# A hybrid decoder trunk on one core: which row pairs of a column pair take seven block products, and where three small pieces of work stand in the order

## The chip, the core and the metric

The kernel runs on one core of one Trainium2 chip. The metric is the device time of one execution in microseconds (us). The engines are TensorE (PE in the profile, its weight loads PEld), VectorE (DVE), ScalarE (ACT), GpSimd (POOL) and SyncE (SP, which here only issues DMAs).

## The reference

One sequence of 256 positions with 2048 features goes through two layers in float32. Layer 0 is retention with 8 heads (per head: 256 wide queries and keys, 512 wide values, a decay matrix, a norm, a SiLU gate), then a squared-ReLU MLP 2048 -> 8192 -> 2048. Layer 1 is latent attention with 16 heads, then such an MLP again.

```python
h = rms_norm(x, norm_mix[0]);  x = x + retention(h, ret_w_in, ret_w_out, cos, sin)
x = x + relu(rms_norm(x, norm_mlp[0]) @ w1[0])**2 @ w2[0]
k_nope, k_pe, v = mla_shared_kv(rms_norm(x, kv_norm_in), w_kv_down, ...)   # latent 512 + 64, up-projected
x = x + mla_attention(rms_norm(x, norm_mix[1]), w_dq, w_uq, w_o, k_nope, k_pe, v)
x = x + relu(rms_norm(x, norm_mlp[1]) @ w1[1])**2 @ w2[1]
```

Nearly all of the time is matrix products of the 256 rows with some 470 MB of float32 weights.

## The kernel before, in words

**Split products.** TensorE multiplies in a shorter float format. So each operand is split into a high and a low part (`split`, L164 to L173: ScalarE casts the high part, L167; VectorE subtracts it to get the low part, L168), and each product of a 128x128 with a 128x512 block is three matmuls (L336 to L338): high by high, high by low, low by high.

**Column pairs, eights and sevens.** The large products go by `gemm_pair` (L313): 1024 output columns (two blocks of 512) of all 256 rows (two blocks of 128). It runs over eight row pairs; each row pair is 256 rows of the weights, one DMA of 1 MB, and is worked on by `quad` (L264). A row pair is a 2x2 times 2x2 block product. Plainly that is 8 block products (24 matmuls, "an eight"): the 1 MB is split in two halves, two casts and two subtractions. With Strassen's and Winograd's scheme it is 7 (21 matmuls, "a seven"): then VectorE also adds the four weight blocks into sums u1 to u4 in place (L301, L304, L305), and four pieces are split instead of two (b11 with b22, b21, u1 with u2, u3 with u4; the second is half as long). A seven also needs sums of the blocks of the left operand, made once by `with_sums` (L372) and used by every column pair. `kinds` says which of the eight row pairs, counted from 0, are sevens. Results gather in seven PSUM banks; `pair_out` (L348) copies six of them (ScalarE) and adds them (VectorE), partly one step later.

**Which row pairs are sevens now.** `THREE` = 3, 5, 7; `FOUR` = 1, 3, 5, 7; `HEAD` = 3, 4, 6, 7 (L29). Heads 1 to 7 use HEAD in their gate-and-value pair (L754, named rp). The output projection of retention (ro) uses THREE and FOUR for the first four heads and 5, 7 for the last four. In the MLPs (L758 on) the up-projection (u) has eight column pairs p; p = 2, 4, 6 use FOUR, the others THREE, the first of layer 0 only 5, 7. Hidden features go in four groups: two u pairs, then two column pairs of the down-projection (d), the first with THREE and the second with FOUR; in the last group the first has THREE and the other 1024 columns are two plain products (`gemm`, L386) of one 512-wide block each. After a u pair, `up` (L765) adds the results, applies ReLU, transposes on TensorE, squares, splits, and makes the sums. After a d pair the results are added to the residual stream in HBM by DMA (`to_home`, L124), in the last group to the stream in SBUF (`into_x`, L132).

**Buffers.** 4 of raw weights, 5 of high halves and 5 of low halves (1024 columns each), 4 PSUM banks "acc", 2 "tp", 2 as one "at", 14 of 2 KB.

**Order.** Each chunk of weights is one tick of a clock (`tick`, L63). `later(n, fn)` puts work into a queue that is due n ticks later; `need` (L69) runs the queue until a list is long enough. Engines execute in order.

**Start.** Head 0 is done by plain products (rg, rq, rk, rv); its input blocks come in with the first of them (`start`, L588). The sums for HEAD are made from a second load of x (`again`, L563), due 7 + c ticks after block c came in; before head 1's pair, the queue is drained until all four are there (L752). GpSimd computes the angles of the two rotary tables (`sincos`, L465, some two dozen small steps each): retention's early, the latent attention's (named tm) due 12 ticks after the inputs, and its table (`mla_tables`, L515) 20 ticks after. They depend on positions only. GpSimd also makes each norm's reciprocal root (`rstd`, L142), the one of a head's output among them (`ret_out`, L644: `o_m`, `o_r`), for which VectorE's `y` (L660) waits.

**Between the layers.** `into_next` (L447) adds the last results to x, squares, transposes and scales it for the latent's down-projection (kd, 320 and 256 columns, L873) and the query's (dq). kd does its first block over all four chunks of rows, then its second. Before it, the queue is drained until the norm's root r2 is there (L816).

Of the kernel before, what the change touches and what calls it, by code (L numbers as in the profile page):

```python
# [19 lines left out]

P = 128
NT = 2
S = NT * P
D = 2048
KD = D // P
# [3 lines left out]
NOPE, ROPE, MV, KVR, QR = 128, 64, 128, 512, 1536  # L29
KV_NBS, Q_NB = (320, 256), 384  # L30
GROUPS = (4, 4, 4, 4)
THREE, FOUR, HEAD = (3, 5, 7), (1, 3, 5, 7), (3, 4, 6, 7)
PI = math.pi

G_MIX0, G_MLP0, G_KV, G_MIX1, G_MLP1 = 0, 16, 32, 48, 64
# [15 lines left out]
def yoco(ctx: ExitStack, tc: tile.TileContext, a):  # L51
# [29 lines left out]
    def later(n, fn):  # L81
        queue.append((clock[0] + n, next(count), fn))
# [327 lines left out]
    def x_block_t(blocks, b, g0s, outs, name, sums):  # L410

        for k2 in range(2):
            tp = transposed(
                lambda t, j: blocks[t][:, (2 * k2 + j) * P : (2 * k2 + j + 1) * P], f"{name}_tp{b}{k2}"
            )
            for g0, out in zip(g0s, outs):
                scales = [gain(g0 + b * 4 + k2 * 2 + j) for j in range(2)]
                v = act_tile(f"{name}{g0}_{b}{k2}")
                if not sums:
                    split_act(v, tp, scales)  # L420
                    out.append(v)
                elif 2 * b + k2 in FOUR:
                    u = f2k([2, S], f"{name}u_{b}{k2}")
                    for j in range(2):
                        nc.scalar.activation(u[:, j], tp[:, j], AF.Copy, scale=scales[j])
                    split_act(v, u)
                    out.append((v, with_sums(u, f"{name}{b}{k2}")))
                else:
                    split_act(v, tp, scales)
                    out.append((v, None))  # L430
# [31 lines left out]
    c1, c2, c3 = _pi_parts()  # L462
    pos_f = pool.tile([P, NT], F32, name="pos_f")

    def sincos(inv, w, name):  # L465

        n = NT * w

        def f2k(shape, name):
            return shaped(act_tile(name, F32).rearrange("p j i s -> p (j i s)"), shape)  # L470

        ang = f2k([NT, w], f"{name}_ang")
        for t in range(NT):
            nc.gpsimd.tensor_scalar(ang[:, t], inv, pos_f[:, t : t + 1], None, op0=ALU.mult)
        flat = ang.rearrange("p t w -> p (t w)")
        k = f2k([2, n], f"{name}_k")
        for i in range(2):
            nc.gpsimd.tensor_scalar(k[:, i], flat, 1 / (2 * PI), 0.25 * i, op0=ALU.mult, op1=ALU.add)
        nc.gpsimd.tensor_scalar(k, k, MAGIC, -MAGIC, op0=ALU.add, op1=ALU.add)
        kh = f2k([2, n], f"{name}_kh")  # L480
        nc.gpsimd.tensor_scalar(kh, k, MAGIC_HI, -MAGIC_HI, op0=ALU.add, op1=ALU.add)
        kl = f2k([2, n], f"{name}_kl")
        nc.gpsimd.tensor_tensor(kl, k, kh, op=ALU.subtract)
        r = f2k([2, n], f"{name}_rr")
        both = flat.unsqueeze(1).to_broadcast([P, 2, n])
        part = f2k([2, n], f"{name}_part")

        def less(dst, src, kk, c):
            nc.gpsimd.tensor_scalar(part, kk, c, None, op0=ALU.mult)
            nc.gpsimd.tensor_tensor(dst, src, part, op=ALU.subtract)  # L490
# [62 lines left out]
    def first_inputs(c):  # L553

        t = f2k([2, S], f"x0t_{c}")
        nc.sync.dma_start(t, a["xt"][:, 2 * c : 2 * c + 2, :])
        v = act_tile(f"a0_{c}")
        split_act(v, t, [gain(G_MIX0 + 2 * c + j) for j in range(2)])
        act0.append(v)
        sums0.append(None)  # L560
        if c in HEAD:

            def again():  # L563
                t = f2k([2, S], f"x0s_{c}")
                nc.sync.dma_start(t, a["xt"][:, 2 * c : 2 * c + 2, :])

                def sum_up():
                    for j in range(2):
                        nc.scalar.activation(t[:, j], t[:, j], AF.Copy, scale=gain(G_MIX0 + 2 * c + j))
                    sums0[c] = with_sums(t, f"a0s_{c}")  # L570

                later(2, sum_up)

            later(7 + c, again)

    ss0 = [small(NB, f"ss0_{t}") for t in range(NT)]

# [10 lines left out]
    def start(half):  # L588
        first_inputs(half)
        if half == 3:  # L590
            nc.sync.dma_start(pos_i, a["pos"])
            nc.sync.dma_start(cst, a["cst"])
            nc.sync.dma_start(gpe, a["gpe"])
        if half == 5:
            ret_tables()
        if half == 7:
            for b in range(NB):
                later(2 + b, lambda b=b: load_x(b))
            later(6, scale_tables)
            later(12, lambda: mla_sc.append(sincos(cst[:, C_INVM : C_INVM + 32], 32, "tm")))  # L600
            later(20, mla_tables)

    def ret_rope(acc, out, name, wait):

# [39 lines left out]
    def ret_out(h, s, v, gate, y_act):  # L644
# [10 lines left out]
        for t in range(NT):  # L655
            so = small(1, f"so{h}{t}")
            square_sum(o[:, t], so, f"o{h}{t}")
            ro = rstd(so, RDV, 1, f"o{h}{t}")
            y = f2k([512], f"y{h}{t}")
            nc.vector.scalar_tensor_tensor(y, o[:, t], ro, gate[t], op0=ALU.mult, op1=ALU.mult)  # L660
            ys.append(y)

        def turn():
            for k2 in range(2):
# [51 lines left out]
    for h in range(RH):  # L716
# [32 lines left out]
        if h == RH // 2:  # L749
            ret_out_half(0)  # L750
        need(r0, NT)
        while None in [sums0[k] for k in HEAD]:  # L752
            run_first()
        gemm_pair(a["ret_w_gv"], (h - 1) * 8, list(zip(act0, sums0)), [k in HEAD for k in range(8)], f"rp{h}", paired)  # L754
    ret_out_half(1)


    def mlp(layer, act, r, done):  # L758
        w1, w2 = a[f"mlp_w1_{layer}"], a[f"mlp_w2_{layer}"]
        f0 = 0  # L760
        for gi, nf in enumerate(GROUPS):
            hid, blocks = [], []
            last = gi == len(GROUPS) - 1

            def up(c, p, hid=hid, blocks=blocks, last=last):  # L765

                need(r, NT)
                c = summed(c)
# [4 lines left out]
                def turn(i):  # L773
                    for q in (2 * i, 2 * i + 1):
                        name = f"hid{layer}_{p}{q}"
                        tp = transposed(
                            lambda t, j: c[t][q // 2][:, (q % 2 * 2 + j) * P : (q % 2 * 2 + j + 1) * P], f"{name}_tp"
                        )
                        u = f2k([2, S], f"{name}_u")
                        nc.scalar.activation(u, tp, AF.Square)  # L780
                        v = act_tile(name)
                        split_act(v, u)
                        blocks.append((v, with_sums(u, name) if len(blocks) in (THREE if last else FOUR) else None))
                        hid.append(v)

                later(0, lambda: turn(0))
                later(1, lambda: turn(1))

            for p in range(f0 // 2, (f0 + nf) // 2):
                kinds = THREE[not (p or layer) :] if p % 2 or not p else FOUR  # L790
                gemm_pair(
                    w1, p * 8, act, [i in kinds for i in range(8)], f"u{layer}_{p}", lambda c, p=p, up=up: up(c, p)
                )
            if last:
                x_tiles(f"mlp{layer}")
            for p in range(2):
                if last and p:
                    for b in (2, 3):
                        need(hid, 2 * nf)
                        gemm(  # L800
                            a[f"mlp_w2t_{layer}"], (b - 2) * nf, hid, 4 * nf, 512, f"d{layer}_{gi}{b}",
                            lambda acc, b=b: done(b, acc),
                        )
                    continue

                def add(c, p=p, last=last):
                    into_x(done, c, p) if last else to_home(c, p)

                kinds = [i in (FOUR if p else THREE) for i in range(2 * nf)]
                gemm_pair(w2, p * 32 + 2 * f0, blocks, kinds, f"d{layer}_{gi}{p}", add)  # L810
            f0 += nf

    ss = [small(NB, f"ss2_{t}") for t in range(NT)]
    act_kv, act_q, r2 = [], [], []
    mlp(0, act, r, into_next(ss, [G_KV, G_MIX1], [act_kv, act_q], r2, "n2"))
    need(r2, 2)  # L816


    def pe_rope(dst, u, src, t, i, heads):
# [334 lines left out]
```

## Time and profile before

| what | us |
|---|---|
| three runs | 2496.07, 2493.91, 2493.17; median 2493.91 |
| the profiled execution, its own time | 2494.54 |
| span from its first to its last instruction | 2492.8 |
| TensorE busy / VectorE busy | 2466.3 / 2146.8 |
| retention, to the start of the first MLP | 0 to 745 |
| first MLP | 745 to 1428 |
| latent attention | 1428 to 1809 |
| second MLP | 1809 to 2490 |

How to read it: times in the trace are counted from the span's start. A row in order of time gives the start, the length, the engine, the line, what is written and read, and in brackets how long the engine stood idle before and what ended that. A row of a stretch gives its length and the busy time of each engine in it, then the granted clock of TensorE (1.00 is full), the busy share of the DMA engines and GB/s. The length of a matmul overlaps with the next; what counts is start to start. The records of VectorE overlap a little too.

### The profile page before, as it was taken

How to read it: one execution, taken by the hardware profiler on the slowest of the kernel's cores; microseconds unless marked ns; L12 is line 12 of the kernel's file. 1: busy time of each engine (PE TensorE's matmuls, PEld its weight loads, DVE VectorE, ACT ScalarE, POOL GpSimd, SP SyncE). 2: the span in 40 equal slices, each digit the busy share in tenths (PEclk: the TensorE clock that was granted, in tenths of full speed). 3: DMA queues.
4: the chain of work that ended last, by engine and by line, in shares of the span. 5: the costliest groups of instructions: out<-in, count | busy, mean ns of one | idle time of the engine just before them, and what ended most of it. 6: DMA issues, size and time to landing. Idle time of an engine off the chain costs nothing.

```text
span 2492.8 us, 31703 instructions
## 1 busy us (share of the span) xinstructions
PE 2466.3 (99%) x11644; PEld 2063.3 (83%) x11644; DVE 2146.8 (86%) x2782; ACT 1586.2 (64%) x2241; POOL 248.7 (10%) x308
## 2 busy tenths in 40 slices
PE   9999999999999999999999999999999999999999
PEld 7788888888788888888888888998888888888887
DVE  7798888889899999999999866776689999999996
ACT  6565655556577666667567666576566667576663
POOL 7300011000000020110110101111000201101100
PEclk9999999999999999999999999999999999999999
DMA  8555558456565595685785564445555866856854
GB/s 325 193 188 186 176 190 262 171 190 228 177 217 189 203 262 211 210 263 203 228 270 181 208 219 173 152 139 195 191 180 197 249 222 200 271 197 222 274 193 152
DMA packets 93403, 521.04 MB, mean 209 GB/s; under 512 B 11072, under 2 KB 12224, under 8 KB 40000
## 3 DMA queue, kind: packets, MB, share of 16 engines
q1 hardware_dynamic: 71856, 472.83, 52.4%
q0 software_dynamic: 21248, 46.15, 8.8%
q8 instruction: 91, 1.49, 0.2%
q14 instruction: 64, 0.52, 0.1%
q10 hardware_dynamic: 144, 0.05, 0.0%
HBM read 479.14 MB, written 39.85 MB: 208 GB/s over the span
## 4 chain that ended last, share of the span: by engine, by line
PE 90%; DVE 5%; ACT 3%; POOL 1%; issue 1%; DMA 0%; ACTq 0%; SPq 0%; DVEq 0%; POOLq 0%
PE u_c L336 7%; PE u_c L338 7%; PE u_c L337 7%; PE d_c L337 6%; PE d_c L338 6%; PE d_c L336 6%; PE rq_acc L256 2%; PE rp_c L336 2%; PE rp_c L337 2%; PE rp_c L338 2%; PE rk_acc L256 2%; PE u_p L336 2%; PE u_p L338 2%; PE u_p L337 2%; PE ro_c L338 2%; PE ro_c L336 2%
## 5 line engine op out<-in xcount | busy, mean ns | idle before, releaser
L167 ACT CAST u_wh<-u_raw 128x1024 fp32r<-128x1024 f32 x362 | 342.3, 991 | 213.8 <-DVE u_raw L304 141.7
L167 ACT CAST d_wh<-d_raw 128x1024 fp32r<-128x1024 f32 x352 | 333.4, 994 | 200.0 <-DVE d_raw L304 146.8
L168 DVE TENSOR_TENSOR u_wl<-u_raw,u_wh 128x1024 fp32r<-128x1024 f32 x362 | 396.9, 1143 | 51.8 <-ACT u_wh L167 50.7
L168 DVE TENSOR_TENSOR d_wl<-d_raw,d_wh 128x1024 fp32r<-128x1024 f32 x352 | 387.2, 1149 | 45.2 <-ACT d_wh L167 44.8
L336 PE MATMUL u_c<-u_wh,n 128*128 128x512 f32 x706 | 276.4, 392 | 0.0
L337 PE MATMUL u_c<-u_wl,n 128*128 128x512 f32 x706 | 275.6, 390 | 0.0
L338 PE MATMUL u_c<-u_wh,n 128*128 128x512 f32 x706 | 274.9, 389 | 0.0
L167 ACT CAST rp_wh<-rp_raw 128x1024 fp32r<-128x1024 f32 (+1 forms) x168 | 158.0, 978 | 128.0 <-DVE rp_raw L304 55.8
L336 PE MATMUL d_c<-d_wh,hid 128*128 128x512 f32 x608 | 238.1, 392 | 0.0
L337 PE MATMUL d_c<-d_wl,hid 128*128 128x512 f32 x608 | 237.5, 391 | 0.0
L338 PE MATMUL d_c<-d_wh,hid 128*128 128x512 f32 x608 | 236.7, 389 | 0.0
L168 DVE TENSOR_TENSOR rp_wl<-rp_raw,rp_wh 128x1024 fp32r<-128x1024 f32 (+1 forms) x168 | 183.1, 1132 | 36.8 <-ACT rp_wh L167 36.8
L338 PEld LDWEIGHTS u_c<-u_wh,n 128*128 128x128 f32 x706 | 132.6, 188 | 27.5
L336 PEld LDWEIGHTS u_c<-u_wh,n 128*128 128x128 f32 x706 | 132.5, 188 | 27.0
L337 PEld LDWEIGHTS u_c<-u_wl,n 128*128 128x128 f32 x706 | 132.6, 188 | 26.7
L338 PEld LDWEIGHTS d_c<-d_wh,hid 128*128 128x128 f32 x608 | 114.2, 188 | 23.5
L336 PEld LDWEIGHTS d_c<-d_wh,hid 128*128 128x128 f32 x608 | 114.2, 188 | 23.5
L337 PEld LDWEIGHTS d_c<-d_wl,hid 128*128 128x128 f32 x608 | 114.2, 188 | 22.9
L132 POOL DMA_DIRECT2D xh<-d_c x48 | 41.6, 867 | 855.5 <-ACT d_c L353 853.6
L167 ACT CAST ro_wh<-ro_raw 128x1024 fp32r<-128x1024 f32 x86 | 83.3, 999 | 59.4 <-PE ro_c L338 31.8
L336 PE MATMUL rp_c<-rp_wh,a 128*128 128x512 f32 x280 | 111.5, 398 | 6.0 <-DVE rk_u L608 4.5
L337 PE MATMUL rp_c<-rp_wl,a 128*128 128x512 f32 x280 | 109.8, 392 | 0.0
(463 smaller groups left out, 6147.4 us busy)
## 6 DMA issues: line engine op xcount, KB each, us to landing
u_raw<-in_mlp_w SPq DMA_DIRECT2D x128, 1024.0 KB, 5.7
d_raw<-in_mlp_w SPq DMA_DIRECT2D x112, 1024.0 KB, 5.2
rp_raw<-in_ret_w_gv SPq DMA_DIRECT2D x56, 1024.0 KB, 4.9
ro_raw<-in_ret_w_out SPq DMA_DIRECT2D x32, 1024.0 KB, 4.9
uq_raw<-in_mla_w_uq SPq DMA_DIRECT2D x24, 768.0 KB, 4.1
rq_raw<-in_ret_w_qk SPq DMA_DIRECT2D x16, 1024.0 KB, 5.7
rk_raw<-in_ret_w_qk SPq DMA_DIRECT2D x16, 1024.0 KB, 4.8
d_raw<-in_mlp_w2t SPq DMA_DIRECT2D x16, 1024.0 KB, 5.8
```

What stands on the lines that cost most here:

```text
L132: nc.gpsimd.dma_start(x_home[t][2 * p + j], part, accum_op=ALU.add)
L167: nc.scalar.copy(h, src)
L168: nc.vector.tensor_tensor(l, src, h.bitcast(F32), op=ALU.subtract)
L256: nc.tensor.matmul(acc[f], wh[:, cols], a.rearrange("p i s -> p (i s)"), start=k == 0, stop=k == nk - 1)
L336: nc.tensor.matmul(dst, ah, bh, start=n == 0, stop=False)
L337: nc.tensor.matmul(dst, ah, bl, start=False, stop=False)
L338: nc.tensor.matmul(dst, al, bh, start=False, stop=n == total[key] - 1)
```

## The change

Four parts:

1. In the MLPs every full u pair (p = 1 to 7) and both d pairs of the first three groups have four sevens, at 3, 4, 6, 7 (`LATE`); the first u pair of layer 0 has 6, 7, that of layer 1 has 4, 6, 7. Sums of hidden tiles and of x are made for these positions.
2. Heads 2 to 7 have their sevens at 2, 4, 6, 7, head 1 at 4, 6, 7; the second loads of x for them come later, each by its own number of ticks, and head 1's pair waits for each block's sums only when it gets to that block (`Pairs`).
3. The latent attention's table is computed after head 0's output root `ro`, tied to it by a zero that is made from it; the table itself 12 ticks after.
4. The last d pair of the first MLP is a column pair with sevens at 3, 5, 7; the second MLP keeps its plain products there. The latent's down-projection runs both column blocks over the first two chunks of rows and then both over the last two, and r2 is asked for only where its results are scaled.

```diff
+class Pairs:
+    def __init__(self, tiles, sums, kinds):
+        self.tiles, self.sums, self.kinds = tiles, sums, kinds
+    def __len__(self):
+        n = 0
+        while n < len(self.tiles) and (n not in self.kinds or self.sums[n] is not None):
+            n += 1
+        return n
+    def __getitem__(self, i):
+        return self.tiles[i], self.sums[i]
...
-THREE, FOUR, HEAD = (3, 5, 7), (1, 3, 5, 7), (3, 4, 6, 7)
+THREE, FOUR, HEAD = (3, 5, 7), (1, 3, 5, 7), (2, 4, 6, 7)
+LATE = (3, 4, 6, 7)
...
-                elif 2 * b + k2 in FOUR:
+                elif 2 * b + k2 in LATE:
...
-            later(7 + c, again)
+            later({2: 21, 4: 15, 6: 17, 7: 18}[c], again)
...
-            later(12, lambda: mla_sc.append(sincos(cst[:, C_INVM : C_INVM + 32], 32, "tm")))
-            later(20, mla_tables)
...
+        if h == 0:
+            no_move, pos = small(1, "no_move"), small(NT, "pos_m")
+            nc.gpsimd.tensor_scalar(no_move, ro, 0.0, None, op0=ALU.mult)
+            nc.gpsimd.tensor_scalar(pos, pos_f, no_move, None, op0=ALU.add)
+            mla_sc.append(sincos(cst[:, C_INVM : C_INVM + 32], 32, "tm", pos))
+            later(12, mla_tables)
...
-        while None in [sums0[k] for k in HEAD]:
-            run_first()
-        gemm_pair(a["ret_w_gv"], (h - 1) * 8, list(zip(act0, sums0)), [k in HEAD for k in range(8)], f"rp{h}", paired)
+        kinds = HEAD if h > 1 else HEAD[1:]
+        gemm_pair(
+            a["ret_w_gv"], (h - 1) * 8, Pairs(act0, sums0, kinds), [k in kinds for k in range(8)], f"rp{h}", paired
+        )
...
+            kinds = THREE if last else LATE
...
-                        blocks.append((v, with_sums(u, name) if len(blocks) in (THREE if last else FOUR) else None))
+                        blocks.append((v, with_sums(u, name) if len(blocks) in kinds else None))
...
-                kinds = THREE[not (p or layer) :] if p % 2 or not p else FOUR
+                sevens = LATE if p else LATE[2 - layer :]
...
-                if last and p:
+                if last and p and layer:
...
-                kinds = [i in (FOUR if p else THREE) for i in range(2 * nf)]
-                gemm_pair(w2, p * 32 + 2 * f0, blocks, kinds, f"d{layer}_{gi}{p}", add)
+                gemm_pair(
+                    w2, p * 32 + 2 * f0, blocks, [i in kinds for i in range(2 * nf)], f"d{layer}_{gi}{p}", add
+                )
...
-    need(r2, 2)
...
     def downed(acc, b):
+        need(r2, NT)
...
-    for b in range(2):
-        gemm(a[f"mla_w_kv_down_{b}"], 0, act_kv, KD, KV_NBS[b], f"kd{b}", lambda acc, b=b: downed(acc, b))
+    first = [accs(n, f"kd{b}") for b, n in enumerate(KV_NBS)]
+    for rows in (range(2), range(2, 4)):
+        for b, n in enumerate(KV_NBS):
+            for g in rows:
+                piece(
+                    a[f"mla_w_kv_down_{b}"], g, first[b], act_kv, g, KD, n, f"kd{b}",
+                    done=(lambda acc, b=b: downed(acc, b)) if g == 3 else None,
+                )
```

More of the change, by code (lines that the diff above doesn't have):

```diff
@@ L463, in yoco, with sincos @@
     pos_f = pool.tile([P, NT], F32, name="pos_f")
-    def sincos(inv, w, name):
+    def sincos(inv, w, name, pos_f=pos_f):
         n = NT * w
@@ L763, in mlp, with up @@
             last = gi == len(GROUPS) - 1
-            def up(c, p, hid=hid, blocks=blocks, last=last):
+            kinds = THREE if last else LATE
+            def up(c, p, hid=hid, blocks=blocks, kinds=kinds):
                 need(r, NT)
@@ L789, in mlp @@
             for p in range(f0 // 2, (f0 + nf) // 2):
-                kinds = THREE[not (p or layer) :] if p % 2 or not p else FOUR
+                sevens = LATE if p else LATE[2 - layer :]
                 gemm_pair(
-                    w1, p * 8, act, [i in kinds for i in range(8)], f"u{layer}_{p}", lambda c, p=p, up=up: up(c, p)
+                    w1, p * 8, act, [i in sevens for i in range(8)], f"u{layer}_{p}", lambda c, p=p, up=up: up(c, p)
                 )
@@ L800, in mlp @@
                         gemm(
-                            a[f"mlp_w2t_{layer}"], (b - 2) * nf, hid, 4 * nf, 512, f"d{layer}_{gi}{b}",
+                            a["mlp_w2t"], (b - 2) * nf, hid, 4 * nf, 512, f"d{layer}_{gi}{b}",
                             lambda acc, b=b: done(b, acc),
@@ L1140 @@
         arrays[f"mlp_w2_{i}"] = _quads(g["mlp_w2"][i])
-        arrays[f"mlp_w2t_{i}"] = _chunks(g["mlp_w2"][i][-512 * GROUPS[-1] :, 1024:], 512)
+    arrays["mlp_w2t"] = _chunks(g["mlp_w2"][1][-512 * GROUPS[-1] :, 1024:], 512)
     arrays = {n: np.ascontiguousarray(v) for n, v in arrays.items()}
```

## The prediction

> **What bounds the kernel now.** I read the page first, then busy time by stretch, then VectorE in order of time inside the MLP, then TensorE where it stands still.
>
> ```profile
> span 2492.8 us, 31703 instructions
> PE 2466.3 (99%) x11644; PEld 2063.3 (83%) x11644; DVE 2146.8 (86%) x2782; ACT 1586.2 (64%) x2241; POOL 248.7 (10%) x308
> PE 90%; DVE 5%; ACT 3%; POOL 1%; issue 1%; DMA 0%; ACTq 0%; SPq 0%; DVEq 0%; POOLq 0%
> ```
>
> TensorE carries the chain that ended last, so fewer products should mean less time. VectorE's 86% is an average over stages, though; in one MLP stretch (down-projection, two column pairs of one group) it reads otherwise:
>
> ```profile
> core 0: us, PE busy (x) PEld busy (x) DVE busy (x) ACT busy (x) POOL busy (x), PEclk, DMA share, GB/s
> 1001.00:1085.00 84.00, 84.00 (x380) 69.32 (x379) 78.83 (x91) 55.84 (x73) 9.37 (x11) 1.00 0.69 223
> 997.40:1040.90 43.50, 43.50 (x200) 35.84 (x200) 41.20 (x51) 31.14 (x42) 0.77 (x1) 1.00 0.52 193
> 1040.90:1081.80 40.90, 40.90 (x182) 33.81 (x181) 37.99 (x41) 25.06 (x31) 7.06 (x9) 1.00 0.86 258
> ```
>
> The last two rows are VectorE's own pair boundaries. The first pair has three sevens and also VectorE's work on the u pair before it (sums, hidden tiles): I call such a pair heavy. The second has four sevens and only a d pair's sums behind it: light. VectorE is busy 41.20 of 43.50 us and 37.99 of 40.90 us. Its remaining 2.3 and 2.9 us are no reserve, as these rows show (start, length):
>
> ```profile
> 1029.01 6.37 DVE L168 TENSOR_TENSOR d_wl<-d_raw,d_wh 128x1024 fp32r<-128x1024 f32 x6 [0.47 <-ACT d_wh L167]
> 1035.30 1.22 DVE L301 TENSOR_TENSOR d_raw<-d_raw 128x1024 f32<-128x1024 f32 x1
> 1036.55 0.69 DVE L304 TENSOR_TENSOR d_raw<-d_raw 128x512 f32<-128x512 f32 x1
> 1037.28 0.69 DVE L305 TENSOR_TENSOR d_raw<-d_raw 128x512 f32<-128x512 f32 x1
> 1038.44 2.36 DVE L168 TENSOR_TENSOR d_wl<-d_raw,d_wh 128x1024 fp32r<-128x1024 f32 x2 [0.47 <-ACT d_wh L167]
> ...
> 435.10 4.10 DVE L168 TENSOR_TENSOR rp_wl<-rp_raw,rp_wh 128x1024 fp32r<-128x1024 f32 x4 [0.58 <-ACT rp_wh L167]
> 439.11 1.22 DVE L301 TENSOR_TENSOR rp_raw<-rp_raw 128x1024 f32<-128x1024 f32 x1
> ...
> 442.25 2.36 DVE L168 TENSOR_TENSOR rp_wl<-rp_raw,rp_wh 128x1024 fp32r<-128x1024 f32 x2 [0.46 <-ACT rp_wh L167]
> ```
>
> Every seven ends with a wait of 0.47 us: L304 makes u2, ScalarE must cast it, and L305 is shorter than that cast.
>
> **The price of one seven.** On VectorE: two sevens side by side start 442.25 - 435.10 = 7.15 us apart. A seven and an eight take 1038.44 - 1029.01 = 9.43 us, so an eight takes 2.28, and making an eight a seven adds 4.87 us (4.4 work, 0.47 wait). On TensorE it takes away three matmuls:
>
> ```profile
> 1049.83 0.39 PE L336 MATMUL d_p<-d_wh,hid 128*128 128x512 f32 x1
> 1050.05 0.39 PE L337 MATMUL d_p<-d_wl,hid 128*128 128x512 f32 x1
> 1050.28 0.39 PE L338 MATMUL d_p<-d_wh,hid 128*128 128x512 f32 x1
> 1050.51 0.39 PE L336 MATMUL d_c<-d_wh,hid_more 128*128 128x512 f32 x1
> ```
>
> 1050.51 - 1049.83 = 0.68 us. From the code, before has 28 sevens in the heads, 11 in ret_out, 26 + 27 in the u pairs and 24 + 24 in the d pairs: 140. After: 27, 11, 30 + 31, 30 + 27: 156. Sixteen more take 10.9 us from TensorE and put 16 x 4.87 = 78 us on VectorE: one more in each of fourteen heavy pairs, three in the first MLP's last pair, one fewer in head 1.
>
> **Heavy pairs** (u pairs 1, 3, 5, 7 and the first d pair of three groups, two layers: 14). VectorE needs 41.20 + 4.4 + 4 x 0.47 = 47.5 us, and its other waits (about 0.9 us at the pair's end, behind ScalarE's copies of the sums) may stay. TensorE would need 43.5 - 0.68. VectorE sets the pair: 47.6 - 43.5 = +4.1 each, **+57**. Bounds: -0.68 each (-10, everything hidden) and +4.8 each (+67). The hidden tiles' sums only change sides (one for a group's first u pair, three for its second).
>
> **Light pairs** (12) keep four sevens, but move them from 1, 3, 5, 7 to 3, 4, 6, 7. The heads' pairs run those very positions today:
>
> ```profile
> 403.02 0.39 PE L336 MATMUL rp_c<-rp_wh,a 128*128 128x512 f32 x1
> ...
> 441.26 0.39 PE L338 MATMUL rp_c<-rp_wh,a 128*128 128x512 f32 x1
> 442.26 0.73 PE L336 MATMUL rp_p<-rp_wh,a0s_more 128*128 128x512 f32 x2 [0.62 <-ACT rp_wh L167]
> 443.21 0.50 PE L336 MATMUL rp_c<-rp_wh,a 128*128 128x512 f32 x1 [0.22 <-ACT rp_wh L167]
> ...
> 445.69 0.61 PE L256 MATMUL rq_acc<-a,rq_wh 128*128 128x512 f32 x2
> ```
>
> That pair takes 445.69 - 403.02 = 42.67 us for 180 matmuls that need 180 x 0.2267 = 40.81. It loses 1.9: two sevens in a row take VectorE 14.3 us and TensorE 2 x 21 x 0.2267 = 9.5, and the five buffers of split weights hold too little lead for that (lead: how long before TensorE uses a split half VectorE has made it). I take +1.9 each, **+23** (bounds 0 and +26). No lead is left for the heavy pair that follows, so its cost stands in full.
>
> **The other MLP pairs.** Last group's first d pair (three sevens as before) now starts without a lead: +1.5 twice. The first u pair of each layer has sevens 6 and 7 side by side: +0.5 twice. Both are estimates, parts of the light pair's 1.9. **+4** (0 to +8).
>
> **Last pair of the first MLP.** Three sevens replace a plain product of two blocks: -2.0 on TensorE.
>
> ```profile
> 1383.00:1428.00 45.00, 45.00 (x211) 37.04 (x210) 35.80 (x54) 29.34 (x55) 3.25 (x6) 1.00 0.56 197
> 1428.00:1455.00 27.00, 27.00 (x204) 26.90 (x203) 17.58 (x28) 18.31 (x35) 3.07 (x6) 1.00 0.71 241
> L171 DVE SCALAR_TENSOR_TENSOR n<-n_tp,gains,n 128x256 fp32r<-128x256 f32 x24 | 10.9, 478 | 2.5 <-ACT n L170 2.3
> ```
>
> VectorE has 9 us there. It gets 3 x 4.87 = 14.6 and 2.4 of pair sums, and loses about 4.4 (block 2's residual and an eighth, 8 of the 24 L171, moves behind the end): 48.2 for 45, +3. Behind it blocks 2 and 3 now arrive together. The reordered down-projection has four of its eight pieces, half of 27 us, to cover a chain of six ScalarE copies, four sums, four residual adds, transposes and eight scalings per block, with their subtractions: I take another +4. **+7** (-2 to +12). The reciprocal root r2 is needed only where `downed` scales, so its moved `need` costs nothing.
>
> **Heads.** Sevens at 2, 4, 6, 7 leave one neighbouring pair instead of two; of the 1.9 lost today I keep 0.15: 6 x -1.75 = **-10.5** (0 to -11.4). In head 1 the latent tables go:
>
> ```profile
> 95.70 0.19 POOL L145 TENSOR_SCALAR o_m<-so 128x1 f32<-128x1 f32 x1
> 96.51 0.47 POOL L490 TENSOR_TENSOR tm_rr<-tm_rr,tm_part 128x128 f32<-128x128 f32 x1
> DVE y L660 <- POOL o_r L147: 6.9, 2, 5.0
> 97.39 0.88 PE L187 MATMUL ytp<-cst,y 128*128 128x128 f32 x6 [1.29 <-DVE y L660]
> 110.01 0.50 PE L336 MATMUL rp_c<-rp_wh,a 128*128 128x512 f32 x1 [4.45 <-DVE rk_u L608]
> 105.00:115.00 10.00, 5.55 (x18) 4.08 (x17) 9.53 (x18) 6.53 (x11) 1.96 (x3) 0.83 0.70 261
> ```
>
> GpSimd runs the tables' steps around head 0's root o_m; VectorE waits 5.0 us for o_r and then holds the accumulator that rp needs. TensorE loses 1.3 + 4.5 us, and at a granted clock of 0.83 over ten microseconds another 1.7. Tied to that root, the steps come behind it: the same two dozen small ones on GpSimd and two more that carry the tie, one Sin on ScalarE, sixteen short products on VectorE. Behind them on GpSimd stands only head 1's root, a whole head away, so the added wait delays nobody. The four row-pair sums (ScalarE and VectorE) and their loads on SP, until now drained ahead of head 1's pair, are spread over its quads, of which one fewer is a seven (+0.7); the loads stand in SP's order with the weights', four buffers ahead. 7.5 - 0.7 plus 1.2 for the stalls that a seven fewer spares: **-8** (0 to -10).
>
> **Sum.** 57 + 23 + 4 + 7 - 10.5 - 8 = +72.5 on the profiled execution's 2494.5: 2567.0; the median shown lies 0.6 lower: **2566.4 us**.
>
> **Rivals.** (1) *VectorE absorbs it, faster*: if ordering fills ScalarE's waits, a stretch needs 78.83 + 4.4 = 83.2 us of 83.3 and TensorE stays the bound: 2494 - 10.9 - 18.5 = 2465. For it: TensorE never waits in the MLP today. Against: no seven in the rows above had its wait filled. It decides from where a stretch's waits stay under 0.1 us. Chance 0.13. (2) *Light pairs lend to heavy ones*: if the waits at the pairs' ends vanish and light pairs do not stall, a stretch takes 78.83 + 4.4 + 8 x 0.47 = 87.0 us, +3.0 instead of 4.1 + 1.9: 12 x 3.0 + 2 x 4.1 + 11 - 18.5 = +37, 2531. For it: the light pair's 37.99 of 40.90 leaves 1 us beside its four waits. Against: the heads' pairs stall at these positions today. Chance 0.17; 0.03 of it comes down to no difference. (3) *The clock falls too*:
>
> ```profile
> 1646.06 0.66 PE L187 MATMUL qptp<-cst,qpp 128*128 128x128 f32 x4 [1.88 <-DVE ot L168]
> 1643.00:1651.00 8.00, 6.12 (x37) 5.84 (x36) 5.17 (x12) 5.81 (x11) 2.31 (x1) 0.79 0.57 199
> ```
>
> A wait of 1.88 us was enough for a granted clock of 0.79 over the next 8 us, 1.7 us lost; a heavy pair's longest stall, at the second of two neighbouring sevens, I work out as 7.15 - 21 x 0.2267 = 2.4. Unless VectorE is then late anyway, 14 x 1.7 = +24: 2590. Chance 0.09. The Trainium skill (TensorE: Matmul & The Clock Gate, What's actually happening) says that the clock halves after an idle window of about 3.4 us; by that rule no heavy pair's stall would do it and this rival would be empty. The trace disagrees, with 1.88 us. That the sevens do not appear at all is no case: they are written out by index.
>
> **Chances.** Forecast 0.61 (its own range 2535 to 2588), rivals 0.13, 0.17, 0.09. Range 2505 to 2596: it leaves out rival 1, the low end of 2 and the top of 3. Within 0.2%, about what a measurement of this kernel can tell from no change, 0.03; faster 0.13; slower 0.84.
>
> **What would show it.** After the change the MLP stretches should be 88 to 92 us with VectorE over 93% busy and TensorE waiting for u_wh and d_wh; heads 2 to 7 shorter by about 1.7 each; no 4.5 us wait at 110; L660's wait for GpSimd under 2.5 us in head 0. I am wrong if VectorE fits into 83 us of a stretch, that is if L305's wait is filled, or if light pairs run at 40.9.

## The result, and the profile after

The kernel after takes 2562.16 us (median of 4 runs, 2560.70 to 2566.43); the kernel before, run beside it, 2494.07 (2493.17 to 2496.07). The ratio is 1.0275, 95% interval 1.0257 to 1.0293: 68.1 us slower.

Line numbers of this part move by 19: the casts are L186, the subtractions L187, the sums of a seven L320, L323, L324, the three matmuls L355 to L357. First the page of after, its span, busy times and chain:

```profile
span 2558.9 us, 31824 instructions
PE 2484.0 (97%) x11596; PEld 2043.5 (80%) x11596; DVE 2219.8 (87%) x2870; ACT 1605.1 (63%) x2279; POOL 249.2 (10%) x310
PE 73%; DVE 18%; ACT 6%; issue 2%; POOL 0%; DMA 0%; ACTq 0%; SPq 0%; DVEq 0%; POOLq 0%
```

VectorE's part of the chain went from 5% to 18%, while its share of the span rose by one point only. TensorE now waits, and these are its two largest sums of waits (us in total, times, longest):

```profile
PE d_p L355 <- ACT d_wh L186: 23.9, 24, 1.9
PE u_p L355 <- ACT u_wh L186: 18.8, 22, 1.0
```

The same group of the first MLP as in the prediction, at VectorE's pair boundaries (first the heavy d pair, its light one, then a light u pair and a heavy one):

```profile
1001.05:1049.92 48.87, 44.56 (x198) 34.85 (x196) 46.74 (x61) 32.87 (x46) 2.41 (x3) 1.00 0.55 183
1049.92:1093.11 43.19, 42.28 (x184) 33.85 (x183) 38.32 (x41) 24.90 (x31) 6.59 (x9) 1.00 0.78 238
1093.11:1135.99 42.88, 41.98 (x182) 33.38 (x181) 38.31 (x40) 24.89 (x31) 4.94 (x6) 1.00 0.77 239
1135.99:1182.20 46.21, 43.84 (x196) 34.48 (x194) 44.11 (x52) 31.59 (x44) 0.00 (x0) 1.00 0.51 183
```

The heavy pairs are 48.87 and 46.21 long, 47.54 in the mean (47.6 predicted; d has three of the hidden sums, u one). VectorE fills some 95% of them. The light pairs are 43.19 and 42.88, 2.1 over the 40.90 of before, and VectorE is *not* full there: 38.3, as before (37.99). Why they are longer all the same is seen in the light u pair. VectorE first, in order of time:

```profile
1100.18 4.09 DVE L187 TENSOR_TENSOR u_wl<-u_raw,u_wh 128x1024 fp32r<-128x1024 f32 x4
1104.19 1.22 DVE L320 TENSOR_TENSOR u_raw<-u_raw 128x1024 f32<-128x1024 f32 x1
...
1107.33 1.22 DVE L187 TENSOR_TENSOR u_wl<-u_raw,u_wh 128x1024 fp32r<-128x1024 f32 x1 [0.47 <-ACT u_wh L186]
1108.77 1.23 DVE L187 TENSOR_TENSOR u_wl<-u_raw,u_wh 128x1024 fp32r<-128x1024 f32 x1 [0.22 <-ACT u_wh L186]
1111.49 1.83 DVE L187 TENSOR_TENSOR u_wl<-u_raw,u_wh 128x1024 fp32r<-128x1024 f32 x2 [1.49 <-ACT u_wh L186]
...
1116.38 6.37 DVE L187 TENSOR_TENSOR u_wl<-u_raw,u_wh 128x1024 fp32r<-128x1024 f32 x6 [0.47 <-ACT u_wh L186]
```

Then ScalarE and TensorE of the same pair:

```profile
1110.41 1.05 ACT L186 CAST u_wh<-u_raw 128x1024 fp32r<-128x1024 f32 x1 [1.67 <-PE u_c L357]
...
1111.75 0.39 PE L356 MATMUL u_c<-u_wl,n 128*128 128x512 f32 x1
...
1133.14 0.73 PE L355 MATMUL u_p<-u_wh,n_more 128*128 128x512 f32 x2 [0.61 <-ACT u_wh L186]
```

The subtraction that ends at 1100.18 + 4.09 = 1104.27 makes what TensorE takes at 1111.75: a lead of 7.5 us. More is not to be had there: VectorE's 1.49 before 1111.49 is a wait for ScalarE, and ScalarE's 1.67 before 1110.41 a wait for TensorE to give a buffer back. VectorE stands idle in the early part of the pair because the buffers are full, and at 1133.14, three sevens later, TensorE waits for it. Spare time cannot be stored beyond what the buffers hold, 7.5 us in this pair.

Where the 2558.9 - 2492.8 = 66.1 us of the two spans lie (from the first matmul of each stage to that of the next, in the last row to the last matmul):

| stage | before | after |
|---|---|---|
| head 1, its rq to the end of rp | 78.8 | 71.4 |
| heads 2 to 7, six pairs | | -7.9 together |
| u stretch, full (six) | 84.35 | 89.5 |
| d stretch, full (six) | 84.35 | 91.6 (one 93.2) |
| first u stretch of each MLP | 87.5, 85.9 | 90.4, 88.9 |
| last d stretch, first MLP | 90.0 | 86.1 |
| kd | 26.5 | 31.4 |
| uq | 133.2 | 131.6 |
| last d stretch, second MLP | 87.2 | 87.4 |

One half clock falls into the 93.2 of after, and one into the 133.2 of before (last section).

### The profile page after: what moved, and what is told of

Its sections match the earlier page's. It is cut to its first block, busy times and chain, and to the rows that moved or that the text cites. A ratio compares the mean times of both kernels' runs of the same rounds, so it can differ in the third digit from the quotient of the medians.

```text
span 2558.9 us, 31824 instructions
## 1 busy us (share of the span) xinstructions
PE 2484.0 (97%) x11596; PEld 2043.5 (80%) x11596; DVE 2219.8 (87%) x2870; ACT 1605.1 (63%) x2279; POOL 249.2 (10%) x310
## 3 DMA queue, kind: packets, MB, share of 16 engines
q8 instruction: 91, 1.49, 0.2%
## 4 chain that ended last, share of the span: by engine, by line
PE 73%; DVE 18%; ACT 6%; issue 2%; POOL 0%; DMA 0%; ACTq 0%; SPq 0%; DVEq 0%; POOLq 0%
PE u_c L355 5%; PE u_c L356 5%; PE u_c L357 5%; PE d_c L355 4%; PE d_c L357 4%; PE d_c L356 4%; DVE d_wl L187 4%; DVE u_wl L187 3%; PE rp_c L355 2%; PE rp_c L356 2%; PE rp_c L357 2%; PE rq_acc L275 2%; PE rk_acc L275 2%; ACT u_wh L186 2%; ACT d_wh L186 2%
## 5 line engine op out<-in xcount | busy, mean ns | idle before, releaser
L187 DVE TENSOR_TENSOR u_wl<-u_raw,u_wh 128x1024 fp32r<-128x1024 f32 x378 | 410.8, 1133 | 60.6 <-ACT u_wh L186 60.4
L186 ACT CAST u_wh<-u_raw 128x1024 fp32r<-128x1024 f32 x378 | 351.0, 985 | 152.2 <-DVE u_raw L323 100.0
L186 ACT CAST d_wh<-d_raw 128x1024 fp32r<-128x1024 f32 x370 | 344.2, 987 | 162.6 <-DVE d_raw L323 115.0
L187 DVE TENSOR_TENSOR d_wl<-d_raw,d_wh 128x1024 fp32r<-128x1024 f32 x370 | 403.4, 1137 | 48.1 <-ACT d_wh L186 47.7
L355 PE MATMUL u_c<-u_wh,n 128*128 128x512 f32 x658 | 256.6, 397 | 4.7 <-ACT u_wh L186 4.7
L356 PE MATMUL u_c<-u_wl,n 128*128 128x512 f32 x658 | 257.5, 391 | 0.0
L357 PE MATMUL u_c<-u_wh,n 128*128 128x512 f32 x658 | 256.5, 390 | 0.0
L186 ACT CAST rp_wh<-rp_raw 128x1024 fp32r<-128x1024 f32 (+1 forms) x166 | 159.0, 981 | 146.9 <-DVE rp_raw L323 73.1
L355 PE MATMUL d_c<-d_wh,hid 128*128 128x512 f32 x618 | 242.7, 397 | 3.9 <-ACT d_wh L186 3.9
L357 PE MATMUL d_c<-d_wh,hid 128*128 128x512 f32 x618 | 240.8, 390 | 0.0
L187 DVE TENSOR_TENSOR rp_wl<-rp_raw,rp_wh 128x1024 fp32r<-128x1024 f32 (+1 forms) x166 | 182.5, 1136 | 31.0 <-ACT rp_wh L186 29.5
L355 PEld LDWEIGHTS u_c<-u_wh,n 128*128 128x128 f32 x658 | 123.5, 188 | 38.6 <-ACT u_wh L186 14.3
L356 PEld LDWEIGHTS u_c<-u_wl,n 128*128 128x128 f32 x658 | 123.6, 188 | 27.8 <-DVE u_wl L187 3.1
L355 PEld LDWEIGHTS d_c<-d_wh,hid 128*128 128x128 f32 x618 | 116.2, 188 | 35.2 <-ACT d_wh L186 12.4
L357 PEld LDWEIGHTS u_c<-u_wh,n 128*128 128x128 f32 x658 | 123.5, 188 | 25.6
L357 PEld LDWEIGHTS d_c<-d_wh,hid 128*128 128x128 f32 x618 | 116.2, 188 | 24.5
L186 ACT CAST ro_wh<-ro_raw 128x1024 fp32r<-128x1024 f32 x86 | 83.1, 998 | 59.7 <-PE ro_c L357 31.4
L355 PE MATMUL rp_c<-rp_wh,a 128*128 128x512 f32 x286 | 112.0, 392 | 1.1 <-DVE rk_u L625 1.1
L357 PE MATMUL rp_c<-rp_wh,a 128*128 128x512 f32 x286 | 111.4, 390 | 0.0
```

The costliest lines, as they stand in the source:

```text
L186: nc.scalar.copy(h, src)
L187: nc.vector.tensor_tensor(l, src, h.bitcast(F32), op=ALU.subtract)
L355: nc.tensor.matmul(dst, ah, bh, start=n == 0, stop=False)
L356: nc.tensor.matmul(dst, ah, bl, start=False, stop=False)
L357: nc.tensor.matmul(dst, al, bh, start=False, stop=n == total[key] - 1)
```

## The experiments

Twelve kernels ran, each beside the kernel before on the same chip (2494.6 to 2495.9 there; its interval is in the ratio). By these intervals a difference between two of the changed kernels is good to some 6 us.

**The heads alone.** The kernel before with parts 2 and 3.

```diff
-THREE, FOUR, HEAD = (3, 5, 7), (1, 3, 5, 7), (3, 4, 6, 7)
+THREE, FOUR, HEAD = (3, 5, 7), (1, 3, 5, 7), (2, 4, 6, 7)
...
+            mla_sc.append(sincos(cst[:, C_INVM : C_INVM + 32], 32, "tm", pos))
```

> The kernel before with parts 2 and 3 alone (heads' sevens at 2, 4, 6, 7, head 1 at 4, 6, 7, the sums of x spread out, latent's tables tied to head 0); MLPs, last pair and kd as before. If the parts add up as the trace of after suggests, the first MLP starts near 729 instead of 745 and everything behind is as before: 2494 - 15.6 = 2478 us. Rival: the time saved in retention is lent (loads start earlier and collide, or the half-clock at 1646 moves), and less than 8 us arrive at the end: over 2486.

Measured: 2479.55, ratio 0.993 (0.9918 to 0.9943), 15.8 less. All that retention wins arrives at the end.

**The last pair alone.** The kernel before with part 4.

```diff
-                if last and p:
+                if last and p and layer:
...
```

> The kernel before with part 4 alone (the first MLP's last d pair as a column pair with sevens at 3, 5, 7; kd's order; r2 asked for later). The prediction gave this part +7 (+3 inside the pair, +4 behind it). Trace of after reads -4.0 for the stretch and +4.9 for kd, with other parts changed around it: about +1, 2493 to 2497. If the prediction's +3 inside the pair holds when the pair ahead of it is not changed: 2499 to 2503.

Measured: 2494.99, ratio 0.9996 (0.9988 to 1.0005): nothing. By difference, and if the parts add, part 1 costs 68.1 + 15.8 + 0.4 = 84.3, good to some 6. Why the two halves cancel shows in the transposes of the norm (tile n_tp; PE, weight loads, VectorE, ScalarE), the last stretch and kd, before:

```profile
1338.29:1428.33 90.04, 3.48 (x24) 2.76 (x24) 10.90 (x24) 10.67 (x24) 1.00 0.54 194
1428.33:1454.79 26.46, 1.04 (x8) 0.93 (x8) 3.66 (x8) 3.55 (x8) 1.00 0.72 245
```

and with part 4 alone:

```profile
1338.82:1424.93 86.11, 1.03 (x8) 0.93 (x8) 3.67 (x8) 3.58 (x8) 1.00 0.54 188
1424.93:1454.44 29.51, 3.70 (x24) 2.78 (x24) 11.12 (x24) 10.84 (x24) 1.00 0.75 256
```

Sixteen transposes (2.5 us of TensorE) and as many scalings (7 us of VectorE) moved from the stretch into kd. The stretch is 3.9 shorter, kd 3.0 longer. VectorE over the same two places (the pair, then kd), as total busy time in the third pair of numbers:

```profile
1381.00:1425.00 44.00, 44.00 (x199) 36.29 (x198) 42.85 (x55) 30.24 (x47) 2.17 (x4) 1.00 0.56 192
1425.00:1454.50 29.50, 29.20 (x218) 28.22 (x217) 26.79 (x51) 25.35 (x57) 4.14 (x8) 1.00 0.75 257
```

In kd it went from 17.58 of 27.00 to 26.79 of 29.50: 9.2 moved there, where the prediction had moved 4.4. So the pair fitted.

**Other positions, same count.** The kernel after with one neighbouring pair of sevens instead of two.

```diff
-LATE = (3, 4, 6, 7)
+LATE = (2, 4, 6, 7)
```

> The kernel after with sevens at 2, 4, 6, 7 instead of 3, 4, 6, 7 in all MLP column pairs: the same count, one neighbouring pair of sevens instead of two. My theory (VectorE's total work plus its 0.47 us wait in each seven bounds an MLP stretch, 87 us or more): only the light pairs' extra 2 us can go, 12 x 1.9 = 23, so 2538 to 2562. Rival (it is the neighbouring sevens that cost, and the five buffers of split weights; the count alone would fit): stretches come back to about 84, 12 x 6 = 72 less, 2490 to 2505.

Measured: 2547.58, ratio 1.0202 (1.0186 to 1.0217), 14.6 less than after, within the theory's range and far from the rival's. u stretches fell from 89.5 to 87.6, d stretches hardly. At VectorE's boundaries, the two light pairs in the middle of the same group:

```profile
1052.94:1094.37 41.43, 41.35 (x183) 33.86 (x182) 38.30 (x40) 24.86 (x31) 6.59 (x9) 1.00 0.84 249
1094.37:1135.55 41.18, 41.10 (x182) 33.65 (x181) 38.23 (x40) 24.77 (x31) 4.94 (x6) 1.00 0.81 249
```

They were 43.19 and 42.88, and 40.90 in before: one neighbouring pair of sevens less gives back 1.7 of the 2.0 to 2.3 that a light pair had lost. The heavy u pairs stay at 46.2. The heavy d pairs do not gain: five of six have half clocks (last section) and take 49.9 to 51.1, the sixth takes 48.7. So positions explain most of the light pairs' loss, and nothing of the heavy pairs'.

**The waits inside a seven.** The kernel after with another order behind the sums, so that ScalarE can cast u1 and u3 under VectorE's last additions.

```diff
...
-        u1, u2 = parts(raw[:, 0:1024], 2, 2)
+        u1, u3 = two(b, 0, 2)
         mm("p5", s(1), u1)
-        mm("p6", s(2), u2)
-        u3, u4 = parts(raw[:, 1024:], 2, 3)
         mm("p7", s(0), u3)
+        u2, u4 = two(b, 1, 3)
+        mm("p6", s(2), u2)
         mm("c21", a(1, 1), u4)
```

> The kernel after with another order inside a seven: behind the sums, u1 and u3 are cast and subtracted as one pair (two casts of 512), then u2 and u4, products p5, p7, p6, then c21's. u1 and u3 are ready one and two additions before u4, so ScalarE casts under VectorE's last additions. If the 0.47 us wait of each seven is what puts a stretch above TensorE's 83.3: eight waits of 0.47 are 3.8 us per stretch, over twelve stretches and the last one some 45 to 50, so 2510 to 2520, and VectorE's share rises above 88%. Rival (VectorE's busy time alone or the positions set the pair): within 8 us of 2562. Rival that the wait only moves (to ScalarE's cast of u2, u4, which then comes late): also about 2562, with a wait of VectorE for the cast of another part.

Measured: 2521.83, ratio 1.0102 (1.0088 to 1.0116), 40.3 less than after, 2 above the range that was expected and far from the rivals, some 2.6 of it in the heads' pairs (42.3 instead of 42.7 each). The wait is gone; VectorE subtracts right behind its last addition:

```profile
1108.64 0.69 DVE L333 TENSOR_TENSOR u_raw<-u_raw 128x512 f32<-128x512 f32 x1
1109.25 2.35 DVE L307 TENSOR_TENSOR u_wl<-u_raw,u_wh 128x1024 fp32r<-128x1024 f32 x2
```

A part came back as a new wait of TensorE, for the part that is now cast last:

```profile
PE d_c L364 <- ACT d_wh L305: 12.9, 18, 1.1
```

**Less work for VectorE.** The kernel after without the last additions of each u pair, or with them on GpSimd.

```diff
-                c = summed(c)
+                c = [[block[0] for block in row] for row in c]
```

> The kernel after, with those four additions of each MLP u pair left out (the hidden features are made from the first of the two blocks alone, so a part of the sum is missing). Theory: 16 x 2.4 = 38 less than 2562, about 2524; the gap between this and the same additions on GpSimd is what GpSimd costs. Rival (positions and buffers): within 8 us of 2562.

Measured: 2535.25, ratio 1.0158 (1.0142 to 1.0173), 26.9 less than after, where 38 was expected: a d and a u stretch together lose 4.2 of VectorE's busy time and 3.6 of their length.

```diff
...
-                c = summed(c)
+                c = summed(c, nc.gpsimd)
```

> The kernel after, with the four additions that end each MLP u pair (the pair's last sums of two blocks) on GpSimd instead of VectorE. Theory (VectorE's busy time plus its waits sets a stretch): 2.4 us less on VectorE for each of sixteen u pairs, all of it on the path: 16 x 2.4 = 38 less than 2562, about 2524. Rival (positions and buffers of the sevens set it, VectorE's total does not): within 8 us of 2562. If GpSimd takes VectorE's time at shared operands, part of the 38 comes back, to be read against the next kernel.

Measured: 2595.69, ratio 1.0409 (1.0391 to 1.0426): 33.5 *more* than after, 60.4 more than with the additions left out. Four groups of this kernel (mean ns of one behind the busy time):

```profile
L388 POOL TENSOR_TENSOR u_c<-u_c,u_v 128x512 f32<-128x512 f32 x16 | 35.3, 2206 | 10.1 <-DVE u_v L378 9.4 <-DMA u_raw<-in_mlp_w 0.7
L379 DVE TENSOR_TENSOR u_p<-u_p,u_u 128x512 f32<-128x512 f32 x16 | 28.5, 1781 | 0.0
L378 DVE TENSOR_TENSOR u_v<-u_p,u_v 128x512 f32<-128x512 f32 x16 | 28.5, 1778 | 0.0
L375 DVE TENSOR_TENSOR u_u<-u_p,u_v 128x512 f32<-128x512 f32 x16 | 11.1, 691 | 0.6
```

and the middle two in the kernel after:

```profile
L378 DVE TENSOR_TENSOR u_v<-u_p,u_v 128x512 f32<-128x512 f32 x16 | 10.9, 684 | 0.0
L379 DVE TENSOR_TENSOR u_p<-u_p,u_u 128x512 f32<-128x512 f32 x16 | 10.9, 683 | 0.0
```

An addition takes GpSimd 2.1 to 2.2 us (the first of each four 1.7) against VectorE's 0.68, and two of VectorE's own, issued while GpSimd's runs, take 1.1 us longer each: 2.2 of the 2.4 saved are lost. The hidden tiles also come later: TensorE's sixteen transposes that start on them wait 11.8 us in all, a wait that after does not have. The Trainium skill (SBUF — State Buffer, SBUF: two separate sides) says that a VectorE operation with two SBUF inputs and a GpSimd one that reads SBUF exclude each other for a whole instruction. The trace agrees: L378 and L379 have both inputs in SBUF and went from 684 to 1780 ns; L375, one input in PSUM and run beside GpSimd's first addition, stayed at 691.

**Which pair has the fourth seven.** Two mirrored kernels: after with three sevens (4, 6, 7) in the heavy pairs, and after with three in the light ones.

```diff
-                sevens = LATE if p else LATE[2 - layer :]
+                sevens = (LATE if p % 2 == 0 else LATE[1:]) if p else LATE[2 - layer :]
...
```

> The kernel after, with three sevens (4, 6, 7) instead of four in the fourteen heavy pairs; light pairs stay at 3, 4, 6, 7. Everything but the MLP's count is as after. The prediction's reading (light pairs stall by 1.9 us at these positions whatever the heavy ones do): 2478 for the heads' part, +1 for the last pair, +6 for the first u pairs, 12 x 1.9 = +23: about 2508. Rival (only VectorE's total of a stretch counts, which is now again that of before, and a pair's stall is made up in the next): 2478 + 7 = 2485.

```diff
-                sevens = LATE if p else LATE[2 - layer :]
+                sevens = (LATE[1:] if p % 2 == 0 else LATE) if p else LATE[2 - layer :]
...
```

> The kernel after, with three sevens (4, 6, 7) in the twelve light pairs instead of four, and four (3, 4, 6, 7) in the fourteen heavy pairs: the mirror of the kernel with three in the heavy pairs, which took 2515.8, and two sevens more in all. The prediction's reading (each pair for itself: a heavy pair with four is VectorE's, 4.1 over before, a light pair with three has TensorE as its bound, +0.7 for the three products it gains and about 0.5 for the neighbours 6 and 7): 2479.5 + 1 + 14 x 4.1 + 12 x 1.2 + 2 = 2554. Rival (a stretch's total on VectorE counts, and a light pair with work to spare wins lead for the heavy one): about as the mirror, 2516 to 2522.

Measured: 2515.76, ratio 1.0081 (1.0066 to 1.0096), with the fourth seven in the light pairs; 2555.33, ratio 1.0246 (1.0230 to 1.0261), with it in the heavy ones. One d and one u stretch in a row, of before, of the former and of the latter (the third number pair is VectorE):

```profile
1000.85:1169.59 168.74, 168.74 (x760) 139.27 (x759) 158.38 (x183) 112.38 (x145) 13.91 (x16) 1.00 0.68 225
```

```profile
903.80:1077.60 173.80, 171.62 (x759) 138.22 (x758) 159.21 (x183) 111.79 (x145) 13.97 (x16) 1.00 0.67 218
```

```profile
912.02:1092.38 180.36, 173.74 (x759) 139.50 (x758) 159.40 (x183) 112.21 (x146) 13.94 (x16) 0.99 0.66 210
```

The same sevens, the same 183 instructions and the same 159 us on VectorE: 168.7, 173.8 or 180.4 us (a half clock adds 1.6 to the last, granted 0.99; three of the six d stretches there go without, and a d and a u stretch then take 178.8). The total of a stretch does not set its length; in which pair and at which positions the work falls does. The prediction's reading (2508 and 2554) was close on both, the rival's (2485, and "as the mirror") failed on both.

**The table alone.** The kernel before with part 3.

```diff
-            later(12, lambda: mla_sc.append(sincos(cst[:, C_INVM : C_INVM + 32], 32, "tm")))
-            later(20, mla_tables)
...
+            mla_sc.append(sincos(cst[:, C_INVM : C_INVM + 32], 32, "tm", pos))
+            later(12, mla_tables)
```

> The kernel before with part 3 alone: the latent attention's table tied to head 0's root, sums of x for the heads as before. The prediction puts the two stalls (1.3 and 4.5) and the half clock (1.7) of head 1 on the table: 2494.1 - 7.5 = 2486.6. Rival (the stalls are those of the four sums of x that are drained ahead of head 1's pair, the table lies beside them): within 2 us of 2494.

Measured: 2490.70, ratio 0.9982 (0.9973 to 0.9991): 3.9 less, between the two. L660 no longer waits 5.0 for o_r, the transposes' wait is gone, but at rp's start and behind it stands:

```profile
106.33 0.50 PE L336 MATMUL rp_c<-rp_wh,a 128*128 128x512 f32 x1 [2.38 <-DVE rk_u L606]
...
105.00:115.00 10.00, 8.67 (x33) 7.10 (x34) 8.20 (x17) 5.03 (x10) 7.85 (x12) 0.83 0.63 217
```

In after the same matmul waits 1.13, and the ten microseconds run at full clock:

```profile
104.53 0.50 PE L355 MATMUL rp_c<-rp_wh,a 128*128 128x512 f32 x1 [1.13 <-DVE rk_u L625]
...
105.00:115.00 10.00, 10.00 (x46) 8.29 (x45) 7.17 (x9) 4.58 (x6) 8.75 (x12) 1.00 0.64 237
```

So the table was the first stall and about half of the second. The rest, and the clock, went only with part 2, which spreads the drained sums of x and takes one seven out of head 1; which of the two did it was not separated.

**All three edits together.**

> The kernel after with three edits together: the other order inside a seven (u1 with u3, then u2 with u4), the u pairs' last additions on GpSimd, and sevens at 2, 4, 6, 7. If the gains add (40 for the order as measured, 38 for the additions, some 15 for the positions), 2562 - 93 = 2469, where TensorE takes over as the bound: it needs 10.9 us less than before in products, so it cannot fall far below 2494 - 15.6 - 10 = 2468. If they overlap, or GpSimd's additions come late for the hidden tiles: 2480 to 2500.

Measured: 2529.49, ratio 1.0139 (1.0124 to 1.0154), far above what was expected: the order alone is better. Without the GpSimd part:

> The kernel after with the other order inside a seven and sevens at 2, 4, 6, 7, the u pairs' last additions on VectorE: the kernel with all three edits (2529.5) less its GpSimd part. If GpSimd's additions lose time here as they did alone (33.5 over the kernel after), this one takes 2529.5 - 33 = 2496 or, where the gains overlap, up to 2510 (2521.8 - 14.6 = 2507 if order and positions add). Rival (the positions are what made the kernel with three edits 7.7 slower than the order alone, and GpSimd costs nothing any more once the waits are gone): about 2529.

Measured: 2519.96, ratio 1.0098 (1.0081 to 1.0115). Neither forecast held: GpSimd costs 9.5 in this setting, not 33, and the positions add nothing clear to the order (1.9). At VectorE's boundaries the light pairs are 1.0 (d) and 0.5 (u) shorter than with the order alone, but the heavy u pairs 1.0 longer, and all six heavy d pairs have half clocks instead of three: the gains do not add.

**The best version.** The heads' parts on the kernel before, with the other order inside a seven (the diffs above).

> The kernel before with parts 2 and 3 (2479.5 measured) and the other order inside a seven (u1 with u3, then u2 with u4). Theory: where TensorE is the bound the spared waits of VectorE are worth nothing, so MLP stretches stay at 84.35 and only the seven heads' pairs, which stall, gain 0.4 each: 2476 to 2478. Rival (the order is better or worse in itself, on ScalarE with one cast more per seven, or in TensorE's waits for c21): a change of over 6 us, mostly in the MLPs.

Measured: 2475.19, ratio 0.9923 (0.9910 to 0.9935), 19.4 less than before: faster than both kernels. Its MLP, a d and a u stretch:

```profile
982.21:1150.87 168.66, 168.66 (x759) 139.27 (x758) 157.95 (x183) 116.05 (x173) 13.92 (x16) 1.00 0.70 225
```

TensorE is busy throughout, and the order, worth about 38 us in the MLPs of after, is worth nothing here; it gained in the heads, where pairs stall. That all MLP pairs take 1, 3, 5, 7 was not tried: by the code, a seven at 1 of a heavy pair holds the two banks that the hidden tiles' transposes need.

## Why the prediction was right, point by point

- **Part 1, predicted 57 + 23 + 4 = 84; 84.3 by difference.** Heavy pairs +4.0 in the mean of the two shown and +3.9 in that of all fourteen (4.1 predicted; its own sum, 47.5 - 43.5, gives 4.0). The mean hides two sizes: the d ones take 48.9 (50.5 with the half clock), the u ones 45.9 to 46.2. Light pairs +2.1 (1.9), mostly from the neighbouring sevens, as the prediction had it. That a seven's wait is not filled was the reason to refuse VectorE's spare 2.3 and 2.9 us; filling it by order gave 40.3 back, 37.7 of it outside the heads. Of the "other MLP pairs" the sign was right only in part: the first u stretches took 2.9 and 3.0 more in place of the 4.6 that the prediction's terms give (0.5 for the first pair, 4.1 for the heavy one), the second MLP's last stretch 0.2 instead of 1.5. These misses, and the d stretches' 7.2, which is over 4.1 + 1.9, cancel, and so do the u stretches' 5.2, which is under it: that the sum agrees to a microsecond is luck.
- **Last pair of the first MLP, predicted +7; nothing measured.** The step that failed is "+3 inside the pair": "loses about 4.4" was too little. The pair sheds 9.2 us of VectorE's work to kd, by the windows above, and 2.5 of TensorE's, so it was 3.9 shorter. (The prediction's terms there add up to 48.4, not 48.2; the +3 does not hang on it.) kd's +4 was right in kind: 3.0 alone, 4.9 in after.
- **Heads 2 to 7, predicted -10.5; -7.9.** Heads 3 to 7 gave 1.6 each, 0.15 less than reckoned. Head 2 gave nothing, for a reason that VectorE's and then TensorE's rows of after show:

```profile
150.92 0.41 DVE L395 TENSOR_TENSOR a0s_sum<-x0s 128x256 f32<-128x256 f32 x1
...
154.72 0.18 DVE L543 SCALAR_TENSOR_TENSOR petab<-tm_sc,gpe 128x32 f32<-128x32 f32 x1
...
156.26 0.18 DVE L546 SCALAR_TENSOR_TENSOR petab<-tm_sc,gpe 128x32 f32<-128x32 f32 x1
156.36 0.68 DVE L388 TENSOR_TENSOR rp_c<-rp_c,rp_p 128x512 f32<-128x512 f32 x1
156.96 0.74 DVE L190 SCALAR_TENSOR_TENSOR vl<-rp_c,n_r,vh 128x512 fp32r<-128x512 f32 x1
```

```profile
157.76 0.50 PE L670 MATMUL o<-vl,sh 128*128 128x512 f32 x1 [1.81 <-DVE vl L190]
```

  The late sums of x and the moved table's sixteen products (petab) stand on VectorE just ahead of head 1's last addition and its low values vl, and TensorE waits 1.8 us for those. With the table alone the products lie at 119.8 to 124.8, and that wait is not there. "The added wait delays nobody" looked at the queue on GpSimd and missed the one on VectorE.
- **Head 1, predicted -8; -7.3.** The size was right, the cause half: the table alone gave 3.9, part 2 the rest.
- **Rival 1** (2465, if the waits are filled) fell on its own condition: with them filled a d and a u stretch took 175.4 (989.2 to 1164.6 in that kernel), not 167: the light pairs take 41.2 and 41.4 there, close to the 40.8 that their matmuls need, but the heavy ones still 47.6 and 45.2 with VectorE 97% busy, and what the light ones spare does not reach them. **Rival 2** (light lends to heavy) fell with the mirrored kernels. **Rival 3** (half clock behind heavy pairs' stalls) happened once in the MLPs of after, not fourteen times; only the six d pairs have a stall near the 2.4 worked out (1.82 to 1.87), the u pairs' longest is 1.0.
- **The total, 2566.4 against 2562.16,** is nearer than its parts: 7 us too much for the last pair stand against 3.3 us that the heads were to save and did not. That is luck too.

## What to carry to other kernels

Where an engine feeds TensorE through a few buffers, its spare time counts only within the lead that they hold: sum its work pair by pair, not stage by stage, and put heavy steps where no other work lies. Price a step with the wait that it carries (here 4.4 of work and 0.47 of wait), and look whether another order fills it before adding more such steps. Where work is moved, list what shares its new place on every engine, VectorE's products and sums as well as the queue that one is thinking of.

## What was unexpected of the hardware

A short stall's effect on the granted clock does not follow from its length. After has eight stalls of 1.81 to 1.90 us: six at the second of the neighbouring sevens of the heavy d pairs, one behind head 1 (at 157.76, above), one at uq. One of them halved it (the spacing of 512-wide matmuls, start to start, goes to 0.43 from 0.227), seven left it alone:

```profile
848.03 0.73 PE L355 MATMUL d_p<-d_wh,hid_more 128*128 128x512 f32 x2 [1.83 <-ACT d_wh L186]
...
849.68 0.63 PE L357 MATMUL d_p<-d_wh,hid_more 128*128 128x512 f32 x1
850.11 0.63 PE L356 MATMUL d_p<-d_wl,hid_more 128*128 128x512 f32 x1
```

With sevens at 2, 4, 6, 7 a shorter stall of 1.58, with one of 0.89 two microseconds ahead of it, was enough in five of six heavy d pairs:

```profile
1019.05 0.73 PE L355 MATMUL d_p<-d_wh,hid_more 128*128 128x512 f32 x2 [0.89 <-ACT d_wh L186]
1021.36 0.79 PE L355 MATMUL d_c<-d_wh,hid 128*128 128x512 f32 x1 [1.58 <-ACT d_wh L186]
...
1019.00:1029.00 10.00, 8.21 (x21) 5.95 (x22) 10.00 (x14) 6.06 (x8) 0.00 (x0) 0.66 0.41 136
```

The stall at uq (1.87 to 1.91 in every profile) was followed by a half clock in before and in some experiments, not in after or the best version. The Trainium skill (TensorE: Matmul & The Clock Gate, What's actually happening) has the activity judged over a free-running window of 3413 ns. The traces agree: each half clock lasts 3413 ns or twice that (but for one at each kernel's end), and within one profile the starts lie whole multiples of that apart. With sevens at 2, 4, 6, 7 they are 160.78, 843.44, 1020.93, 1201.84, 1939.12 and 2120.03: 200, 52, 53, 216 and 53 windows. Cut at such times, the window of after's halved stall and the next, then the window with the most idle time around the other seven:

```profile
846.13:849.54 3.41, 1.36 (x5) 0.73 (x5) 2.91 (x4) 2.61 (x3) 0.00 (x0) 1.00 0.36 149
849.54:852.96 3.42, 3.42 (x9) 2.65 (x9) 3.42 (x4) 2.75 (x4) 0.00 (x0) 0.50 0.40 117
1948.64:1952.05 3.41, 1.74 (x8) 1.12 (x6) 3.09 (x4) 0.90 (x1) 0.00 (x0) 1.00 0.73 298
```

TensorE is idle 2.05 us of the first window, and the next runs at half clock; it is idle 1.67 of the third, because the stall of 1.87 reaches into the window after, and the clock stays. With sevens at 2, 4, 6, 7 the five halved d pairs have 1.98 to 2.27 us of idle time in one window and the sixth 1.65. The stall of 1.81 behind head 1 lies whole in one window there and halves the clock; in after it falls 0.69 and 1.12 into two and does not. So in these two kernels it is the idle time within one window that counts, not the stall's length, and no stall shown in this section is as long as a window. How much idle time is too much stays open: in before 1.88 us were enough at uq and not in the window from 104.02, and with the other order inside a seven 1.33 us by the records were enough in three of six heavy d pairs.
